# Moving the bias tile in front of the x tiles in a decoder-layer kernel

## The chip, the cores and the metric

The kernel runs on one core of one Trainium2 chip. The metric is the device time of one execution in microseconds (us): 1431.13 us, the median of three runs (1430.40 to 1431.53).

## What is computed

One decoder layer for 512 rows of 2048 values, in float32. One combined projection feeds three attention branches and three merge gates; the branches are projected back, gated, summed, projected once more and normalised:

```python
h = x @ w_in + b_in                       # 2048 -> 11528 columns
o_fox, o_swa, o_moba = fox(...), swa(...), moba(...)   # 8 heads of 64 each
br_i = (merge_heads(o_i) * silu(z_i)) @ w_branch_i     # 512 -> 2048, three times
y = sum_i sigmoid(gate_i) * br_i
out = y @ w_out                           # 2048 -> 2048
return layer_norm(alpha * x + out, ln_g, ln_b)
```

## The kernel before

**Number format.** Each float32 operand of a product is split into an upper part and a lower part, both of type float32r. A product of two split operands is three matmuls: upper by upper, upper by lower, lower by upper. A weight block of 128 partitions by 512 columns has the parts `hi` and `lo` (lines 132 and 135). x has `xh` and `xl`, the gated attention output `ozh` and `ozl`, and the mixed result y has `yh` and `yl`, which take over the buffers of `xh` and `xl` (tags `bigh` and `bigl`).

**The stream.** 452 weight blocks go through the kernel in one fixed order. They are loaded two at a time, and block i + 2 is split while block i is multiplied. In front of them stand two passes over the v columns. TensorE's work is this, with the stationary operand (the one loaded into the array) first:

- v passes, lines 272 to 274: a 128-column slice of `xh` or `xl` stays, 324 columns of `hi` or `lo` stream.
- projection `h`, lines 471 to 473: a 128-column slice of `hi` or `lo` stays, 512 columns of `xh` or `xl` stream. 81 tiles of 16 steps of three matmuls. The first 33 tiles belong to the attention branches, the last 48 are gates.
- moba v, lines 490 to 493: a slice of `xh` or `xl` stays, 256 columns of `hi` or `lo` stream.
- branch projections `br`, line 599: a slice of `hi` or `lo` stays, 512 columns of `ozh` or `ozl` stream. 36 matmuls follow each three gate tiles, and 72 stand at the end.
- output `o`, lines 650 to 652: a slice of `yh` or `yl` stays, 512 columns (in the last row tile 256) of `hi` or `lo` stream. The last eight blocks are kept in tiles of their own, `wh` and `wl`.

Attention runs in small steps put between the blocks of `h` and moba v: scores (lines 356 and 357, 96 units), transposes (line 398) and value products (line 417, 24 heads).

**Where tiles lie.** A pool's tiles are placed one behind the other in each partition, in the order of their first allocation, each rounded up to 32 bytes; a pool starts where the one before it ends. The pools are `keep`, `stage`, `ozy`, and behind them `const` and `work`, which give way first to `mix` and then to `last`. In `keep` stand `xh` and `xl` (32 KB each), `bT` and three tiles of 2 KB. `bT` holds the biases, 81 values per partition, 324 bytes, which take 352. All tiles of `stage` (raw blocks, `hi`, `lo`) and `ozy` are 2 KB or 4 KB. `ozh` and `ozl` (24 KB each) are the first tiles of `mix`. So, modulo 2 KB, everything in `stage`, `ozy` and the named tiles of `mix` lies 352 bytes behind `xh` and `xl`. In the built program `xh`, `xl`, `yh` and `yl` are at 128 modulo 2048, `hi`, `lo`, `ozh` and `ozl` at 480, and `wh` and `wl` at 928. A slice of 128 columns starts a multiple of 512 bytes further on.

PSUM has three accumulators of tag `acc` and five of tag `att`. `h` uses `acc`, `br` uses `att`, and `o` uses both.

Of the kernel before, what the change touches and what calls it, by code (L numbers as in the profile page):

```python
# [8 lines left out]
F32 = mybir.dt.float32  # L9
# [4 lines left out]
P = 128  # L14
# [14 lines left out]


def tile_columns():
    """Start columns of the 128-wide tiles of w_in whose product is kept transposed."""
    cols = []
    for p in range(4):
        cols += [FOX_Q + P * p, FOX_K + P * p, FOX_Z + P * p]
    cols.append(SWA_K)
    for p in range(4):
        cols += [SWA_Q + P * p, SWA_Z + P * p]
    for p in range(4):
        cols += [MOBA_Q + P * p, MOBA_K + P * p, MOBA_Z + P * p]  # L40
    for dt in range(KD):
        cols += [g + P * dt for g in GATES]
    return cols


# column ranges of the two v passes that run behind the loads of x
V_CHUNKS = (
    ((FOX_V, 320), (FOX_F, 4)),
    ((FOX_V + 320, 192), (SWA_V, 128), (FOX_F + 4, 4)),
# [2 lines left out]


def weight_stream():
    """The 512-column weight blocks in the order in which they are used."""
    ids = []
    t = 0

    def proj(n):
        nonlocal t  # L60
        for _ in range(n):
            ids.extend(("h", t, c) for c in range(4))
            t += 1

    proj(12)
    proj(1)
    for p in range(4):
        proj(2)
        if p % 2 == 1:
            ids.extend(("v", p // 2, g) for g in range(8))  # L70
    proj(12)
    proj(3)
    for dt in range(KD):
        if dt + 1 < KD:
            proj(3)
        ids.extend(("b", dt, b) for b in range(3))
    ids.extend(("o", ec, k) for ec in range(4) for k in range(KD))
    return ids
# [3 lines left out]
def hybrid_kernel(ctx: ExitStack, tc: tile.TileContext, a: dict, out: bass.AP):  # L82
# [4 lines left out]
    keep = ctx.enter_context(tc.tile_pool(name="keep", bufs=1))  # L87
# [4 lines left out]
    work = att_ctx.enter_context(tc.tile_pool(name="work", bufs=2))  # L92
# [10 lines left out]
        nc.scalar.activation(hi, raw, AF.Copy)  # L103
        nc.vector.tensor_sub(lo, raw, hi.bitcast(F32))  # L104

    # ---- the stream of weight blocks: loaded two at a time, split two blocks ahead of their use
    ids = weight_stream()
    raws, parts = {}, {}
    held = {}
# [8 lines left out]
            nc.sync.dma_start(raws[j], a["ws"][j])  # L118

    def prepare(i):  # L120
        """Rounds block i to its upper part; the step that is returned makes the lower part."""
        if i >= len(ids) or i in parts:
            return None
        load(i // 2)
        raw = raws[i // 2][:, (i % 2) * S:(i % 2 + 1) * S]
        if i in held:
            hi, lo = held[i]
        else:
            hi = stage.tile([P, S], F32R, tag="hi", name="hi")
            lo = stage.tile([P, S], F32R, tag="lo", name="lo")  # L130
        parts[i] = (hi, lo)
        nc.scalar.activation(hi, raw, AF.Copy)  # L132

        def lower():
            nc.vector.tensor_sub(lo, raw, hi.bitcast(F32))  # L135
            for d in range(1, raw_bufs):
                load(i // 2 + d)

        return lower

    # ---- x and the first two v passes
    xh = keep.tile([P, KD, S], F32R, tag="bigh", name="xh")
    xl = keep.tile([P, KD, S], F32R, tag="bigl", name="xl")
    bT = keep.tile([P, 81], F32, name="bT")
    sinkc = const.tile([P, NH], F32, name="sinkc")
    nsink = const.tile([P, NH], F32, name="nsink")
    vfox = const.tile([P, 4, NH, P], F32R, tag="v", name="vfox")
# [16 lines left out]
            nc.sync.dma_start(vraw[n][:, :2 * NV], a["wv"][n])  # L164

    def prepare_v(n):
        """Step n of 32: one block of the v columns, and one of x in the first pass."""
        hi = stage.tile([P, S], F32R, tag="hi", name="hi")
        lo = stage.tile([P, S], F32R, tag="lo", name="lo")
        split(vraw[n // 2][:, (n % 2) * NV:(n % 2 + 1) * NV], hi[:, :NV], lo[:, :NV])  # L170
        if n == 0:
            for c in (slice(0, 256), slice(256, S)):
                nc.vector.tensor_copy(xh[:, 0, c], xraw[0][:, c])
                nc.vector.tensor_sub(xl[:, 0, c], xraw[0][:, c], xh[:, 0, c].bitcast(F32))
        elif n < KD:
            split(xraw[n], xh[:, n], xl[:, n])
        vparts[n] = (hi, lo)
# [4 lines left out]
    load_v(1)  # L182
    load_v(2)

    # products of zeros wake the tensor engine while the first loads run
    warm = stage.tile([P, S], F32R, tag="hi", name="warm")
    nc.vector.memset(warm.bitcast(F32), 0.0)
    wacc = att_tile("warm")
# [39 lines left out]
                                 dst[:, st, h0:h0 + nh, :HD].bitcast(F32))  # L228

    def forget_bias():  # L230
        """8 times minus the running sum of the log-sigmoid; log1p(e) = 2 atanh(e / (2 + e))."""
        nlf = const.tile([P, 32], F32, name="nlf")
        fl = flog.rearrange("p a b -> p (a b)")
        t0 = const.tile([P, 32], F32, name="t0")
        t1 = const.tile([P, 32], F32, name="t1")
        t2 = const.tile([P, 32], F32, name="t2")
        nc.vector.scalar_tensor_tensor(t0, fl, -1.0, fl, op0=ALU.mult, op1=ALU.max)
        nc.scalar.activation(t0, t0, AF.Exp, scale=-1.0)
        nc.vector.tensor_scalar(t1, t0, 2.0, None, op0=ALU.add)
        nc.vector.reciprocal(t1, t1)  # L240
        nc.vector.tensor_mul(t0, t0, t1)
        nc.vector.tensor_mul(t1, t0, t0)
        nc.vector.tensor_scalar(t2, t1, 2.0 / 15.0, 2.0 / 13.0, op0=ALU.mult, op1=ALU.add)
        for c in (11, 9, 7, 5, 3, 1):
            nc.vector.tensor_mul(t2, t2, t1)
            nc.vector.tensor_scalar(t2, t2, 2.0 / c, None, op0=ALU.add)
        nc.vector.tensor_mul(t2, t2, t0)
        nc.vector.tensor_scalar(t1, fl, 0.0, None, op0=ALU.min)
        nc.vector.tensor_sub(nlf, t2, t1)
        pair = work.tile([P, 4, P], F32R, tag="L", name="pair", bufs=3)  # L250
        nc.gpsimd.memset(pair.bitcast(F32), 0.0)
        n3 = nlf.rearrange("p (a b) -> p a b", b=NH)
        nc.scalar.activation(pair[:, :, :NH], n3, AF.Copy)
        nc.vector.tensor_sub(pair[:, :, 32:32 + NH], n3, pair[:, :, :NH].bitcast(F32))
        return pair
# [38 lines left out]
        if KD + 1 <= n < KD + 5:  # L294
            v_evac(0, n - KD - 1, fox_dests[0])

    # ---- attention, in steps that run between the blocks of the projections
    halves = (slice(0, HD), slice(HD, P))

    def q_upper(acc, t, res):  # L300
# [129 lines left out]
    oz = []  # L430

    def plan_pair(kind, p, base, spacing, q, k, z, v):
        """Puts the steps of two heads into the slots from base on."""
        oz.append(z)
        for e in range(2):
            h = 2 * p + e
            g = p // 2 if kind == "swa" else e
            env = {"q": q, "k": k, "z": z, "v": v, "vh": g if kind == "swa" else h, "e": e, "g": g}
            first = base + int(4 * e * spacing)
            at(first - (4 if kind == "fox" else 0), 0, table_for, kind, h, env)  # L440
            for i in range(4):
                s = base + int((4 * e + i) * spacing)
                u = {}
                a_ = (kind, h, i, env, u)
                at(s, 8, unit_scores, *a_)
                at(s + 1, 0, unit_max, *a_)
                at(s + 1, 5, unit_exp, *a_)
                at(s + 2, 1, unit_norm, *a_)
                at(s + 3, 8, unit_turn, *a_)
                at(s + 4, 1, unit_upper, *a_)  # L450
                at(s + 4, 6, unit_lower, *a_)
            at(s + 6, 8, head_values, kind, h, env)
            at(s + 7, 2, head_low, kind, h, env)
            at(s + 7, 7, head_out, kind, h, env)
        return s + 7

    # ---- the parts of the stream
    where = {}
    for i, (kind, t, c) in enumerate(ids):
        where.setdefault((kind, t), i)  # L460
# [52 lines left out]
        nc.vector.tensor_sub(d[:, :, HD:], r, d[:, :, :HD].bitcast(F32))  # L513

    def evac(t, res, *steps):
        """The steps after tile t of the projection: slots after its last one, order there, function."""
        ends[t] = [(*x, res) for x in steps]

    Q = ((1, 2, q_upper), (2, 2, q_lower))
# [2 lines left out]
    t = 0  # L522
# [118 lines left out]
    oacc = {}  # L641

    def out_mm(st, k, hi, lo, half=None):
        """One block of the output product; half: only these 256 columns, in a bank of their own."""
        sl = slice(st * P, (st + 1) * P)
        o = oacc[st]
        if half is not None:
            cs = slice(half * 256, (half + 1) * 256)
            o, hi, lo = oacc[3 + half][:, :256], hi[:, cs], lo[:, cs]
        nc.tensor.matmul(o, yb["h"][:, k, sl], hi, start=(k == 0), stop=False)  # L650
        nc.tensor.matmul(o, yb["l"][:, k, sl], hi, start=False, stop=False)  # L651
        nc.tensor.matmul(o, yb["h"][:, k, sl], lo, start=False, stop=(k == KD - 1))  # L652
# [23 lines left out]
                at(i + 1, 1, residual, ec, st, oacc[st])  # L676

    def norm(st, middle=None):
        """Layer norm of one row tile: columns up to cut on VectorE, the others on ScalarE and GpSimdE."""
        last = st == 3  # L680
        cut = 1536 if last else 1024
        mv = box["last"].tile([P, 5], F32, tag="mv", name="mv", bufs=2)
# [35 lines left out]
            nc.sync.dma_start(rows[:, 2 * S:cut], z[:, 2 * S:cut])  # L718
        nc.sync.dma_start(rows[:, cut:], z[:, cut:])

    # ---- extra work at given slots
    for st in range(4):
        at(st, 3, v_evac, 1, st, fox_dests[1])
    nl = {}
# [93 lines left out]
```

## Time and profile before

| | |
|---|---|
| three runs | 1430.40, 1431.13, 1431.53 us |
| span of the profiled execution | 1429.3 us (1.8 us less than the median run) |
| TensorE matmuls | busy 1409.2 us, 99%, 6659 matmuls |
| weight loads | busy 1167.2 us, 82% |
| VectorE, ScalarE, GpSimd | 45%, 39%, 10% |
| granted TensorE clock, mean | 0.996 of full speed |

The busy time of a matmul (0.39 to 0.40 us at 512 columns) overlaps that of the next, which starts some 0.23 us after it. What a stream of matmuls costs is therefore read from start to start, and called the period here.

### The profile page before, as it was taken

How to read it: one execution, taken by the hardware profiler on the slowest of the kernel's cores; microseconds unless marked ns; L12 is line 12 of the kernel's file. 1: busy time of each engine (PE TensorE's matmuls, PEld its weight loads, DVE VectorE, ACT ScalarE, POOL GpSimd, SP SyncE). 2: the span in 40 equal slices, each digit the busy share in tenths (PEclk: the TensorE clock that was granted, in tenths of full speed). 3: DMA queues.
4: the chain of work that ended last, by engine and by line, in shares of the span. 5: the costliest groups of instructions: out<-in, count | busy, mean ns of one | idle time of the engine just before them, and what ended most of it. 6: DMA issues, size and time to landing. Idle time of an engine off the chain costs nothing.

```text
span 1429.3 us, 17708 instructions
## 1 busy us (share of the span) xinstructions
PE 1409.2 (99%) x6659; PEld 1167.2 (82%) x6659; DVE 636.7 (45%) x1273; ACT 556.8 (39%) x1024; POOL 150.1 (10%) x216
## 2 busy tenths in 40 slices
PE   9999999999999999999999999999999999999995
PEld 8988888898988888888888888888888888888884
DVE  5466656544554555442233333233333323632348
ACT  4355566555545556532222222222222222422231
POOL 1001212332321222100000000000000000000005
PEclk9999999999999999999999999999999999999998
DMA  7333223222222222232323323233232332362322
GB/s 240 116 102 102 82 89 95 75 79 89 79 74 89 89 74 75 81 96 89 103 89 93 99 89 104 89 92 100 89 103 89 92 100 89 119 249 91 101 74 118
DMA packets 41157, 142.37 MB, mean 100 GB/s; under 512 B 4632, under 2 KB 5144, under 8 KB 40304
## 3 DMA queue, kind: packets, MB, share of 16 engines
q1 hardware_dynamic: 40048, 134.58, 30.1%
q0 software_dynamic: 1024, 6.67, 1.2%
q8 instruction: 52, 0.85, 0.2%
q14 instruction: 33, 0.27, 0.1%
HBM read 137.02 MB, written 4.21 MB: 99 GB/s over the span
## 4 chain that ended last, share of the span: by engine, by line
PE 97%; DVE 2%; DMA 1%; SPq 0%; DVEq 0%; issue 0%; ACT 0%
PE h L471 21%; PE h L473 21%; PE h L472 21%; PE br L599 9%; PE o L651 4%; PE o L650 4%; PE o L652 4%; PE o L417 2%; PE pt L398 2%; PE mv L490 1%; PE mv L492 1%; PE mv L493 1%; PE s L357 1%; PE s L356 1%; PE vc L273 1%; PE vc L272 1%
## 5 line engine op out<-in xcount | busy, mean ns | idle before, releaser
L132 ACT ACTIVATE hi<-raw 128x512 fp32r<-128x512 f32 x444 | 280.2, 631 | 740.9 <-PE h L472 464.6
L135 DVE TENSOR_TENSOR lo<-raw,hi 128x512 fp32r<-128x512 f32 x444 | 312.7, 705 | 565.3 <-ACT hi L132 556.7
L471 PE MATMUL h<-xh,hi 128*128 128x512 f32 x1296 | 515.3, 398 | 0.0
L473 PE MATMUL h<-xh,lo 128*128 128x512 f32 x1296 | 513.9, 397 | 0.0
L472 PE MATMUL h<-xl,hi 128*128 128x512 f32 x1296 | 513.3, 396 | 0.0
L473 PEld LDWEIGHTS h<-xh,lo 128*128 128x128 f32 x1296 | 244.0, 188 | 59.4 <-DVE lo L135 0.3
L472 PEld LDWEIGHTS h<-xl,hi 128*128 128x128 f32 x1296 | 244.3, 188 | 55.8
L471 PEld LDWEIGHTS h<-xh,hi 128*128 128x128 f32 x1296 | 244.0, 188 | 55.4
L393 POOL TENSOR_SCALAR lt<-lt,st 128x128 f32<-128x128 f32 (+2 forms) x96 | 70.1, 730 | 309.7 <-DVE st L392 308.0
L651 PE MATMUL o<-hi,yl 128*128 128x512 f32 (+1 forms) x232 | 90.7, 391 | 0.0
L650 PE MATMUL o<-hi,yh 128*128 128x512 f32 (+1 forms) x232 | 89.6, 386 | 0.0
L652 PE MATMUL o<-lo,yh 128*128 128x512 f32 (+1 forms) x232 | 89.2, 384 | 0.0
L599 PE MATMUL br<-ozl,hi 128*128 128x512 f32 x192 | 74.9, 390 | 0.0
L599 PE MATMUL br<-ozh,hi 128*128 128x512 f32 x192 | 74.8, 390 | 0.0
L599 PE MATMUL br<-ozh,lo 128*128 128x512 f32 x192 | 74.7, 389 | 0.0
L631 POOL DMA_DIRECT2D z<-in_xn x4 | 2.2, 550 | 642.1 <-DVE yl L104 642.1
L387 ACT ACTIVATE lt<-lt,st 128x128 f32<-128x128 f32 (+3 forms) x96 | 51.4, 536 | 23.4 <-DVE st L392 10.4
L650 PEld LDWEIGHTS o<-hi,yh 128*128 128x128 f32 x232 | 43.5, 188 | 10.6
L652 PEld LDWEIGHTS o<-lo,yh 128*128 128x128 f32 x232 | 43.5, 188 | 9.6
L651 PEld LDWEIGHTS o<-hi,yl 128*128 128x128 f32 x232 | 43.6, 188 | 9.4
L405 ACT ACTIVATE pth<-pt 128x128 fp32r<-128x128 f32 (+2 forms) x96 | 38.6, 402 | 15.0 <-PE pt L398 14.2
L409 DVE TENSOR_TENSOR ptl<-pt,pth 128x128 fp32r<-128x128 f32 (+2 forms) x96 | 43.4, 452 | 1.0 <-ACT pth L405 0.7
(156 smaller groups left out, 1430.4 us busy)
## 6 DMA issues: line engine op xcount, KB each, us to landing
raw<-in_ws SPq DMA_DIRECT2D x226, 512.0 KB, 3.5
rawv<-in_wv SPq DMA_DIRECT2D x15, 324.0 KB, 3.2
xraw<-in_xT SPq DMA_DIRECT2D x16, 256.0 KB, 5.7
z<-in_xn POOLq DMA_DIRECT2D x4, 1024.0 KB, 9.8
out<-z SPq DMA_DIRECT2D x7, 512.0 KB, 2.6
row<-forget_rows SPq DMA_DIRECT2D x8, 256.0 KB, 3.8
ln_gain<-in_ln_gain POOLq DMA_DIRECT2D x1, 1024.0 KB, 17.9
ln_bias<-in_ln_bias POOLq DMA_DIRECT2D x1, 1024.0 KB, 20.3
```

The source lines that it names most:

```text
L132: nc.scalar.activation(hi, raw, AF.Copy)
L135: nc.vector.tensor_sub(lo, raw, hi.bitcast(F32))
L387: nc.scalar.activation(full[:, :m], full[:, :m], AF.Exp, bias=st[:, 0:1], scale=-1.0, accum_out=st[:, 1:2])
L393: nc.gpsimd.tensor_scalar(lt, lt, st[:, 3:4], 1.0, op0=ALU.mult, op1=ALU.mult)
L409: nc.vector.tensor_sub(env["ptl"][:, c], u["pt"][:, :u["n"] // P], env["pth"][:, c].bitcast(F32))
L471: nc.tensor.matmul(accs[t], hi[:, cc], xh[:, k], start=(k == 0), stop=False)
L472: nc.tensor.matmul(accs[t], hi[:, cc], xl[:, k], start=False, stop=False)
L473: nc.tensor.matmul(accs[t], lo[:, cc], xh[:, k], start=False, stop=(k == KD - 1))
L599: nc.tensor.matmul(br, w[:, cc], o[:, 4 * b + kt], start=(kt == 0 and n == 0), stop=(kt == 3 and n == 2))
L650: nc.tensor.matmul(o, yb["h"][:, k, sl], hi, start=(k == 0), stop=False)
L651: nc.tensor.matmul(o, yb["l"][:, k, sl], hi, start=False, stop=False)
L652: nc.tensor.matmul(o, yb["h"][:, k, sl], lo, start=False, stop=(k == KD - 1))
```

## The change

The tile `bT` is allocated as the first tile of the pool `keep`, no longer behind `xh` and `xl`. In the built program `bT` is then at 128 modulo 2048, and `xh`, `xl`, `yh` and `yl` at 480, where `hi`, `lo`, `ozh` and `ozl` have been and stay. `wh` and `wl` stay at 928. No other tile moves. The instructions of every engine, their order and their shapes are the same before and after, row for row. The rest of the diff turns comments and docstrings into empty lines and is left out here.

```diff
+    bT = keep.tile([P, 81], F32, name="bT")
     xh = keep.tile([P, KD, S], F32R, tag="bigh", name="xh")
     xl = keep.tile([P, KD, S], F32R, tag="bigl", name="xl")
-    bT = keep.tile([P, 81], F32, name="bT")
     sinkc = const.tile([P, NH], F32, name="sinkc")
```

## Rows read from the trace of the kernel before

**Rows 1.** The page: busy time by engine (us, share, instructions), and PE's shares by slice.
```profile
PE 1409.2 (99%) x6659; PEld 1167.2 (82%) x6659; DVE 636.7 (45%) x1273; ACT 556.8 (39%) x1024; POOL 150.1 (10%) x216
...
PE   9999999999999999999999999999999999999995
...
PEclk9999999999999999999999999999999999999998
```

**Rows 2.** Waits of PE and PEld: waiter, waited for: us in total, times, longest.
```profile
PE warm L190 <- DVE warm L187: 1.5, 1, 1.5
PE va L272 <- ACT xh L103: 0.7, 1, 0.7
PE va L273 <- DVE xl L104: 0.5, 2, 0.3
...
PEld h L473 <- DVE lo L135: 0.3, 1, 0.3
```

**Rows 3.** The chain that ended last, gate stage: start us, us, what.
```profile
713.26 8.19 PE br L599 x36
...
755.18 8.19 PE br L599 x36
...
1216.22 16.35 PE br L599 x72
```

**Rows 4.** Timeline of PE where br begins: start us, us, engine, line, operation, tiles.
```profile
713.10 0.39 PE L599 MATMUL br<-ozh,hi 128*128 128x512 f32 x1
713.33 0.40 PE L599 MATMUL br<-ozl,hi 128*128 128x512 f32 x1
713.57 0.39 PE L599 MATMUL br<-ozh,lo 128*128 128x512 f32 x1
...
714.26 0.39 PE L599 MATMUL br<-ozh,lo 128*128 128x512 f32 x1
...
715.85 0.39 PE L599 MATMUL br<-ozh,hi 128*128 128x512 f32 x1
```

**Rows 5.** Timeline of PE in the output product, 180 matmuls apart.
```profile
1284.91 0.39 PE L650 MATMUL o<-hi,yh 128*128 128x512 f32 x1
...
1326.91 0.39 PE L650 MATMUL o<-hi,yh 128*128 128x512 f32 x1
```

**Rows 6.** Groups by line and form: xcount | busy us, mean ns | idle before.
```profile
L471 PE MATMUL h<-xh,hi 128*128 128x512 f32 x1296 | 515.3, 398 | 0.0
...
L650 PE MATMUL o<-hi,yh 128*128 128x512 f32 x216 | 85.1, 394 | 0.0
...
L490 PE MATMUL mv<-hi,xh 128*128 128x256 f32 x128 | 36.6, 286 | 0.0
...
L272 PE MATMUL vc<-hi,xh 128*128 128x324 f32 x64 | 20.1, 314 | 0.0
...
L650 PE MATMUL o<-wh,yh 128*128 128x512 f32 x24 | 9.5, 395 | 0.0
```

**Rows 7.** Timeline of PE in the v passes, 192 matmuls apart.
```profile
23.80 0.31 PE L272 MATMUL va<-hi,xh 128*128 128x324 f32 x1
...
52.59 0.31 PE L272 MATMUL vc<-hi,xh 128*128 128x324 f32 x1
```

**Rows 8.** Timeline of PE in moba v, 23 matmuls apart.
```profile
303.32 0.28 PE L490 MATMUL mv<-hi,xh 128*128 128x256 f32 x1
...
306.07 0.29 PE L493 MATMUL mv<-lo,xh 128*128 128x256 f32 x1
```

**Rows 9.** Groups by line and form: steps that stand between matmuls of h.
```profile
L356 PEld LDWEIGHTS s<-kh,qs 128*128 128x128 f32 x96 | 18.2, 189 | 2.5
...
L423 ACT ACTIVATE otmp<-o 64x512 f32<-64x512 f32 x24 | 14.3, 594 | 2.9 <-PE o L417 2.4
```

**Rows 10.** Groups by line: the splits of the weight blocks.
```profile
L132 ACT ACTIVATE hi<-raw 128x512 fp32r<-128x512 f32 x444 | 280.2, 631 | 740.9 <-PE h L472 464.6
L135 DVE TENSOR_TENSOR lo<-raw,hi 128x512 fp32r<-128x512 f32 x444 | 312.7, 705 | 565.3 <-ACT hi L132 556.7
```

**Rows 11.** Busy time in a stretch of gate tiles: us, count; clock, DMA share, GB/s.
```profile
721.45:755.18 33.73, 33.73 (x145) 27.12 (x145) 9.62 (x14) 8.75 (x15) 0.00 (x0) 1.00 0.30 94
```

**Rows 12.** Timeline of PE at a score step: 384 columns, `kh` and `qs` at equal offsets.
```profile
169.09 0.27 PE L398 MATMUL pt<-ident,lt 128*128 128x128 f32 x1
169.12 0.42 PE L356 MATMUL s<-kh,qs 128*128 128x384 f32 x1
169.38 0.34 PE L357 MATMUL s<-kl,qs 128*128 128x384 f32 x1
169.55 0.40 PE L471 MATMUL h<-xh,hi 128*128 128x512 f32 x1
```

**Rows 13.** Timeline at the end: the last matmul.
```profile
1411.65 0.28 PE L652 MATMUL o<-wl,yh 128*128 128x256 f32 x1
```

## The prediction

> **What bounds the kernel now.** Read the page first: PE is busy 1409.2 of 1429.3 us, every slice but the last shows 9, and its clock is granted in full (9 in all slices but the last) [rows 1]. Then the waits: PE waits 2.7 us for anything in the whole program, all of it in the first microseconds, and its weight loads wait once for a split inside the stream, 0.3 us [rows 2]. So neither a transfer nor another engine holds the stream back. What counts is how long one matmul takes from start to start. Busy time does not tell that, since neighbours overlap; the starts do.
>
> For `h`, take the chain in the gate stage: 36 matmuls of `br` from 713.26, lasting 8.19 us, and the next 36 at 755.18 [rows 3]. Between them are three gate tiles, 144 matmuls, in 755.18 - 713.26 - 8.19 = 33.73 us: a period of 0.2342 us. For `br`, the last group has 72 matmuls in 16.35 us [rows 3]. Its second half, less a first half like the other groups, takes 16.35 - 8.19 = 8.16 us for 36: 0.2267 us. Both kinds have 128x512 operands, three matmuls per step and the same clock. `h` is 3.3% slower.
>
> What sets them apart? Not the array of weights or its buffers: both load `hi` and `lo` from the same tiles. Not the PSUM tag: `o` uses both tags, and its period is (1326.91 - 1284.91) / 180 = 0.2333 us [rows 5], near `h`. What `br` has alone is that its streaming operand (480 modulo 2048) and its stationary operand (480 plus a multiple of 512) lie at equal offsets modulo 512. In `h` they lie 352 bytes apart, in `o` the same with the parts exchanged, and with `wh` and `wl` 800. A second sign is the entry into `br`: the first five periods take (714.26 - 713.10) / 5 = 0.232 us, the next seven (715.85 - 714.26) / 7 = 0.227 [rows 4]. The short period is a rhythm into which streaming and loading fall after some matmuls, and which `h` and `o` never find.
>
> I read this as two reads of the same memory that get in each other's way less often when both walk through it in step. The trace shows the periods, not this cause. The Trainium skill speaks against it: "SBUF — State Buffer", section "Who interferes with whom", gives PE two independent read ports and says that PE never waits on anyone. By that the offset would be worth nothing, and `h` and `br` would have one period; the measured 0.2342 against 0.2267 differ, so the trace does not agree with it as it stands.
>
> **The change, part by part.** No instruction, DMA or wait is added, removed or moved. `bT` itself is read as one value per partition by ScalarE and VectorE, which have time to spare (39% and 45% busy [rows 1]). What changes is that x and y go to 480 modulo 2048. `h`, `o` (but for `wh` and `wl`), moba v and the v passes then have both operands at equal offsets modulo 512, as `br` has now.
>
> 1. Gate tiles of `h`: 48 tiles of 48 matmuls, 2304 in all. Each goes from 0.2342 to 0.2267, saving 0.0075 us: 17.3 us. The rhythm then also runs through the 15 entries into `br` that now cost 8.19 - 8.16 = 0.03 us each: 0.4 us more. Together 17.7 us.
> 2. The other 1296 x 3 - 2304 = 1584 matmuls of `h` [rows 6] would save 11.9 us by the same step. But attention steps break in: 96 score units (mostly with a transpose right before them) and 24 value products [rows 9], up to 120 interruptions. After each the rhythm must be found again; the price is that of the entry into `br`, 0.03 us. 120 x 0.03 = 3.6 us, which leaves 8.3 us. Bounds: 0, if the rhythm never returns in so short a run, and 11.9.
> 3. `o` with `hi` and `lo` at 512 columns: 3 x 216 = 648 matmuls [rows 6], 0.2333 - 0.2267 = 0.0066 us each: 4.3 us. The 72 with `wh` and `wl` [rows 6] go from 800 to 448 bytes apart, unequal before and after: nothing, at most 72 x 0.0066 = 0.5.
> 4. v passes and moba v: 384 matmuls of 324 columns and 384 of 256 (six lines of 64 and three of 128 [rows 6]). Their periods are 28.79 / 192 = 0.150 us [rows 7] and 2.75 / 23 = 0.120 us [rows 8]. No row shows narrower matmuls at equal offsets in a steady run. The upper bound is a saving per column like that of `h`: 0.0047 x 384 = 1.8 and 0.0038 x 384 = 1.4, together 3.2 us. The lower bound is nothing, if what is left over does not shrink with the width. I take the middle, 1.6 us.
>
> The other engines' cover: splits of a block cost ScalarE 0.631 and VectorE 0.705 us [rows 10], against 12 x 0.2267 = 2.72 us for a block of PE's work afterwards, and most of the idle time before the upper split is a wait for PE to free a buffer [rows 10]. A faster PE starts it earlier. If that cover were gone, the 0.3 us wait of [rows 2] shows what a late split costs, once. DMA is busy 30% in the gates at 94 GB/s [rows 11]; 3% more is no load. The tail, from the last matmul at 1411.65 [rows 13] to 1429.3, is VectorE's, GpSimd's and a store's, and stays.
>
> Sum: 17.7 + 8.3 + 4.3 + 1.6 = 31.9 us. The profiled span of 1429.3 becomes 1397.4. The median run is 1431.1, 1.8 above the span, so the time becomes **1399 us**. With every bound at its best (17.7 + 11.9 + 0.5 + 4.3 + 3.2 = 37.6) it is 1393.5.
>
> **The rivals.**
>
> *The offset is not what matters.* The short period of `br` would belong to where `ozh` and `ozl` lie in the whole partition, not modulo 512. For it: no row shows x at another offset. Against it: `o` streams `hi` and `lo`, or `wh` and `wl`, which lie in a distant part of the partition, and both have the same line times (394 and 395 ns [rows 6]); only `br` stands out. Time 1431. By the section of the Trainium skill named above ("SBUF — State Buffer", "Who interferes with whom") nothing would change either, with the same 1431; that rule has [rows 3] against it.
>
> *The rhythm holds only in long undisturbed runs.* Between attention steps there are often only 12 to 18 matmuls of `h`. If the rhythm is not found there, terms 2 and 4 fall to nothing: 17.7 + 4.3 = 22.0 us saved, 1409 us. For it: five periods are lost at each entry into `br` [rows 4], where only one operand changes. Against it: five are a third of such a run, no more.
>
> *Equal offsets collide.* Both reads would hit the same place at the same moment, and the change makes `h` slower. For it: a score matmul whose `kh` and `qs` lie at equal offsets takes 169.38 - 169.12 = 0.26 us for 384 columns, and the next one, of the same width, 0.17 [rows 12]. Against it: a transpose starts 0.03 us earlier and still runs in that time, and `br` has equal offsets and the shortest period of all. As price I take the slowest step of the entry into `br`, 713.57 - 713.33 = 0.24 us [rows 4], an estimate from rows rounded to 0.01. If `h` stayed at 0.24, 3888 x 0.0058 = 22.6 us more: 1454. It decides once the period of `h` rises by 2.9 / 3888 = 0.0007 us.
>
> **How the numbers follow.** A change under 0.2%, 2.9 us, can't be told from none. Chances: the forecast, 1393 to 1405, 0.68; the rhythm only in long runs, 1405 to 1412, 0.14; no effect, 0.12; collision, 0.04; more than my best bounds, 0.02. The range from 1392 to 1412 takes in the first two, with the unknown costs of terms 2 and 4, and leaves out what gives no gain. Faster by over 0.2%: 0.68 + 0.14 + 0.02 = 0.84. Within 0.2%: 0.12. Slower: 0.04.
>
> **What would show it.** In the changed profile, the 144 matmuls of `h` between two groups of `br` should take 32.6 us, not 33.7, and each group of `br` 8.16. 180 matmuls of `o` should take 40.8 us, not 42.0. In the attention stage the starts of `h` should be 0.23 to 0.24 us apart for some five matmuls after a score step and 0.227 after that. PE's waits should stay at a few microseconds. The prediction is wrong if `h` keeps 0.234 (then place or another cause counts), or if new waits of PE for splits or for attention steps eat what the period gives back.

## The result and the profile after

The changed kernel takes 1400.07 us (median of four runs, 1399.89 to 1401.47), the kernel before 1431.24 (median of four). The ratio is 0.9784, with a 95% interval of 0.9772 to 0.9796: 2.2% faster. The profiled execution took 1399.89 us with a span of 1398.1, so 1.8 us lie around the span, as before.

The page of the changed kernel, first its busy times by engine, then the granted clock by slice:

```profile
PE 1377.4 (99%) x6659; PEld 1162.8 (83%) x6659; DVE 636.3 (46%) x1273; ACT 556.8 (40%) x1024; POOL 151.4 (11%) x216
...
PEclk9999999999999999999999999999999999999998
```

Against [rows 1], PE is 31.8 us less busy with the same 6659 matmuls, and VectorE, ScalarE and GpSimd have changed by at most 1.3 us. The clock is granted as before. Its waits (waiter, waited for, us in total, times, longest):

```profile
PE warm L190 <- DVE warm L187: 1.5, 1, 1.5
PE va L272 <- ACT xh L103: 0.8, 1, 0.8
PE va L273 <- DVE xl L104: 0.6, 2, 0.3
...
PEld h L473 <- DVE lo L135: 0.5, 1, 0.5
```

These are the waits of [rows 2], longer by 0.4 us in all. So nothing was won by a wait that went, and no new wait has come. The matmuls themselves follow each other faster. The chain that ended last, at the groups of `br` (start us, us, what):

```profile
618.01 8.16 PE br L599 x36
658.81 8.16 PE br L599 x36
699.61 8.16 PE br L599 x36
...
1189.21 16.32 PE br L599 x72
```

The 144 matmuls of `h` between two groups take 658.81 - 618.01 - 8.16 = 32.64 us: a period of 0.2267, where [rows 3] gave 0.2342. `br` takes 8.16 in every group; its slow entry is gone. In the output product, with 186 matmuls between these two:

```profile
1259.77 0.39 PE L650 MATMUL o<-hi,yh 128*128 128x512 f32 x1
...
1301.93 0.39 PE L650 MATMUL o<-hi,yh 128*128 128x512 f32 x1
```

42.16 / 186 = 0.2267, where [rows 5] gave 0.2333. The last matmul of all now starts here:

```profile
1380.29 0.28 PE L652 MATMUL o<-wl,yh 128*128 128x256 f32 x1
```

The first group of `br` in the kernel before, from the same view as [rows 3]:

```profile
629.44 8.18 PE br L599 x36
```

By stage, with the starts of the first and the last group of `br` as borders:

| stretch | before | after | less |
|---|---|---|---|
| start to the first group of `br` | 629.44 | 618.01 | 11.43 |
| to the last group (14 times 144 `h` and 36 `br`) | 586.78 | 571.20 | 15.58 |
| to the last matmul | 195.43 | 191.08 | 4.35 |
| from there to the end of the span | 17.7 | 17.8 | -0.1 |

### The profile page after: what moved, and what is told of

The parts are those of the page before. It is cut to its first block, busy times and chain, and to the rows that moved or that the text cites. A ratio compares the mean times of both kernels' runs of the same rounds, so it can differ in the third digit from the quotient of the medians.

```text
span 1398.1 us, 17708 instructions
## 1 busy us (share of the span) xinstructions
PE 1377.4 (99%) x6659; PEld 1162.8 (83%) x6659; DVE 636.3 (46%) x1273; ACT 556.8 (40%) x1024; POOL 151.4 (11%) x216
## 4 chain that ended last, share of the span: by engine, by line
PE 96%; DVE 2%; DMA 1%; SPq 0%; issue 0%; ACT 0%; DVEq 0%; ACTq 0%
PE h L471 21%; PE h L473 21%; PE h L472 21%; PE br L599 9%; PE o L651 4%; PE o L650 4%; PE o L652 4%; PE o L417 2%; PE pt L398 2%; PE mv L490 1%; PE mv L492 1%; PE mv L493 1%; PE s L357 1%; PE s L356 1%; DMA xraw<-in_xT 1%; PE vc L274 1%
## 5 line engine op out<-in xcount | busy, mean ns | idle before, releaser
L471 PE MATMUL h<-xh,hi 128*128 128x512 f32 x1296 | 507.4, 392 | 0.0
L473 PE MATMUL h<-xh,lo 128*128 128x512 f32 x1296 | 505.1, 390 | 0.1
L472 PE MATMUL h<-xl,hi 128*128 128x512 f32 x1296 | 505.2, 390 | 0.0
```

The source lines that it names most:

```text
L471: nc.tensor.matmul(accs[t], hi[:, cc], xh[:, k], start=(k == 0), stop=False)
L472: nc.tensor.matmul(accs[t], hi[:, cc], xl[:, k], start=False, stop=False)
L473: nc.tensor.matmul(accs[t], lo[:, cc], xh[:, k], start=False, stop=(k == KD - 1))
```

## The experiments

Four questions were put to the chip: how near must the offsets be; is it the offset between the two operands, or the place of x; what is the rest of a period lost to; and can the attention steps join. A period of `h` below is always that of 144 matmuls between two groups of `br`, as above.

### How near must the offsets be?

Four kernels have the changed order and a gap behind the x tiles, of 64, 32, 8 and 120 values (256, 128, 32 and 480 bytes):

```diff
     xl = keep.tile([P, KD, S], F32R, tag="bigl", name="xl")
+    keep.tile([P, 64], F32, name="gap")
```

> A gap of 256 bytes behind the x tiles moves the weight parts and the attention output on, so that in h, o and the v passes the two operands lie 256 bytes apart modulo 512; br stays at 0. Theory 1 (only equal offsets modulo 512 give the short period): h at 0.233 to 0.235 us, br at 0.2267, time about 1430. Rival (the walk repeats every 256 bytes or less): h stays at 0.2267, time about 1400. Rival (what counts is that x starts at 480 modulo 2048): h stays at 0.2267, time about 1400.

> As gap_256 with 128 bytes. Theory 1: h at 0.233 to 0.235 us, time about 1430. Rival (repeats every 128 bytes): h at 0.2267, time about 1400, and then gap_256 the same. Rival (x at 480 counts): 0.2267, about 1400.

> As gap_256 with 32 bytes, the smallest step of the placing. Theory 1, strict: h at 0.233 to 0.235 us, time about 1430. Theory 1 with some play (near enough to equal is as good): h at 0.2267, time about 1400; gap_480, 32 bytes short of the next 512, then tells whether the play is on one side or both.

> As gap_256 with 480 bytes, that is 32 bytes the other way. Theory 1, strict: h at 0.233 to 0.235 us, time about 1430. With play on both sides: 0.2267 and about 1400, as gap_32. Rival (x at 480 counts): 0.2267, about 1400.

One execution each: 1401.14, 1425.15, 1425.03 and 1426.53 us, in this order; the kernel before took 1431.45 beside them. The chain of gap_256, then of gap_128, gap_32 and gap_480:

```profile
700.76 8.16 PE br L600 x36
741.56 8.16 PE br L600 x36
```

```profile
709.56 8.18 PE br L600 x36
751.32 8.17 PE br L600 x36
```

```profile
708.73 8.18 PE br L600 x36
750.51 8.19 PE br L600 x36
```

```profile
710.10 8.20 PE br L600 x36
751.90 8.20 PE br L600 x36
```

The periods of `h` are 32.64 / 144 = 0.2267, then 33.58 / 144 = 0.2332, and 33.60 / 144 = 0.2333 twice. So 32 bytes to either side cost the rhythm, 128 do, and 256 do not. Equality modulo 512 was too strict: 256 is enough, 128 is not. That x starts at 480 modulo 2048 falls as an explanation, since it did so in all four.

Not every unequal offset costs the whole step. In gap_128 the last eight blocks, `wh` and `wl`, are at 1056 and `yh` and `yl` at 480 in the built program, 64 bytes apart modulo 256. 71 periods lie between these two rows:

```profile
1383.23 0.39 PE L651 MATMUL o<-wh,yh 128*128 128x512 f32 x1
...
1399.49 0.40 PE L653 MATMUL o<-wl,yh 128*128 128x512 f32 x1
```

16.26 / 71 = 0.2290, between 0.2267 and 0.2333. The three slow kernels are still 5 to 6 us faster than the kernel before: 0.2333 is not 0.2342 (3888 x 0.0009 = 3.5 us of that), so which unequal offset it is has an effect of its own.

### The offset, or the place?

One kernel keeps the tile order of before, with the bias tile padded to 512 bytes (of which the kernel uses 81 values, as ever), so that x is at 128 and the weight parts at 640. The other has the order of after, and moves `ozh` and `ozl` alone of the tiles that TensorE reads (two kinds of tiles behind them in `mix`, `sig` and `y`, move along):

```diff
-    bT = keep.tile([P, 81], F32, name="bT")
+    bT = keep.tile([P, 128], F32, name="bT")[:, :81]
```

```diff
+        mix.tile([P, 40], F32, name="gap")
         box["ozh"] = mix.tile([P, 12, S], F32R, name="ozh")
```

> The tile order of before, x at 128 modulo 2048, but the bias tile is padded to 512 bytes, so that the weight parts and the attention output lie at 640, equal to x modulo 512. Theory 1 (the offset between the operands counts): h, o and br at 0.2267 us, time 1400, ratio 0.978. Rival (x has to be at 480, or the bias tile has to stand in front): h stays at 0.234, time 1431, ratio 1.000. Rival (equality modulo 2048 is needed, not 512): 1431 too, with br alone short.

> The changed kernel with a gap of 160 bytes in front of the attention output's split parts, which puts them against the weight parts as x was before the change. Theory 1: br rises to 0.234 us, 576 x 0.0075 = 4.3 us more than the changed kernel, 1404, ratio 0.981; h and o stay at 0.2267. Rival (the place of the attention output in the partition makes br short): br stays at 0.2267 and the time at 1400, ratio 0.978.

Padding alone, with the bias tile where it was: 1400.19 us, ratio 0.9784 (0.9768 to 0.9800), the same as the change. Moving `ozh` and `ozl` away: 1405.29 us, ratio 0.9818 (0.9804 to 0.9833). The chain of the first, then of the second:

```profile
701.06 8.16 PE br L599 x36
741.86 8.16 PE br L599 x36
```

```profile
660.20 8.43 PE br L600 x36
701.28 8.43 PE br L600 x36
...
1194.33 16.86 PE br L600 x72
```

With the padding the period of `h` is 32.64 / 144 = 0.2267. With `ozh` and `ozl` moved, `br` takes 16.86 / 72 = 0.2342 us, the period that `h` had before the change, and `h` stays at (701.28 - 660.20 - 8.43) / 144 = 0.2267. (Its profiled run took 1405.68 us, 5.8 more than that of the changed kernel. Summed from start to start, 4.30 of them are in `br` and 1.34 in the v passes, which come up again below.) The same matmuls get slow or fast with nothing changed but 160 bytes between their operands. This shows the offset as the cause, for `br` by taking it away and for `h` by both ways of making it equal. The place in the partition is out as a rival.

### What is the rest of a period lost to?

The expectations below set a period against 0.2133 us, which is 512 columns at one per cycle of 2.4 GHz. No run here shows a period that short, so this is an assumption of theirs; by it 0.0133 of a period of 0.2267 are the rest, and 0.0209 of one of 0.2342. Two pairs of kernels load and use only 64 of the 128 weight columns in `h`: one pair in the second matmul of each three, the other in all but the first and last step of a tile. Both do so on the kernel before and on the changed one.

```diff
-            nc.tensor.matmul(accs[t], hi[:, cc], xl[:, k], start=False, stop=False)
+            half = slice(j * P, j * P + 64)
+            nc.tensor.matmul(accs[t][:64], hi[:, half], xl[:, k], start=False, stop=False)
```

```diff
+            n = P if k in (0, KD - 1) else 64
+            half, acc = slice(j * P, j * P + n), accs[t][:n]
-            nc.tensor.matmul(accs[t], hi[:, cc], xh[:, k], start=(k == 0), stop=False)
+            nc.tensor.matmul(acc, hi[:, half], xh[:, k], start=(k == 0), stop=False)
...
```

> The changed kernel, in which the second of each three matmuls of h (upper weight part by lower x part) loads and uses only the first 64 of 128 weight columns; half of that product is left out. Theory 1 with its cause (what a period has over 512 columns at full clock, 0.2267 - 0.2133 = 0.0133 us, is lost to the weight load that runs beside the streaming): the period in which the half load runs shrinks by about half of that, 0.0067 us, so 1296 x 0.0067 = 8.7 us less, 1391. Rival (the 0.0133 us belong to the switch from one matmul to the next, whatever is loaded): no period changes, 1400.

> The kernel before, with the same half load; half of that product is left out. There a period has 0.2342 - 0.2133 = 0.0209 us over the 512 columns. Theory 1 with its cause: the period with the half load beside it shrinks by about 0.0104 us, 1296 x 0.0104 = 13.5 us, 1418. Rival (lost to the switch): no period changes, 1431.

> The changed kernel, in which all matmuls of h but those of the first and last step of a tile load and use only 64 of the 128 weight columns (half of those products is left out). Theory 1 with its cause (the time over 512 columns is lost to the load beside the streaming; half_after was slow because loads of two lengths alternated and broke the rhythm): periods of 0.2200 us inside a tile, 3402 x 0.0067 = 22.7 us less, 1377. Rival (lost to the switch of matmuls): 0.2267, 1400. Rival (the rhythm needs loads of full length): 0.230 or more, 1410 or more.

> The kernel before with the same half loads in h. Theory 1 with its cause: the 0.0209 us over 512 columns fall to about half, periods of 0.2238, 3402 x 0.0104 = 35 us less, 1395. Rival (lost to the switch): 0.2342, 1431. If only the conflict of the two reads shrinks and a fixed part stays, something between.

One execution each: 1410.02 and 1423.39 us with one load in three halved, 1409.55 and 1417.22 with all of them. The changed kernel gets 10 us slower by loading less, the kernel before 7 and 14 us faster. With one load in three halved, all three periods of a step rise in the changed kernel, to 0.2289, 0.2304 and 0.2300 on average in the gates, and not only the one beside the half load. In the second pair, the chain of the changed kernel's, then of the other:

```profile
704.15 8.16 PE br L601 x36
745.38 8.16 PE br L601 x36
```

```profile
706.39 8.17 PE br L601 x36
747.73 8.17 PE br L601 x36
```

The loads did become shorter (groups by line, the changed kernel; mean ns of one behind the comma):

```profile
L474 PEld LDWEIGHTS h<-xl,hi 128*64 128x64 f32 x1134 | 152.5, 134 | 101.4
...
L474 PEld LDWEIGHTS h<-xl,hi 128*128 128x128 f32 x162 | 30.5, 188 | 6.0
```

Of 144 matmuls 18 keep the full load. With those at 0.2267 and 0.2342, the other 126 take (33.07 - 18 x 0.2267) / 126 = 0.2301 us in the changed kernel and (33.17 - 18 x 0.2342) / 126 = 0.2298 in the other. Read from start to start, two neighbours with half loads are 0.2300 and 0.2298 us apart, two with full loads 0.2267 and 0.2342, as without the edit. With half loads the offset no longer counts: both stand between the two periods of the full load. My theory that the excess is in proportion to what is loaded falls, and so does its rival, that it belongs to the switch from one matmul to the next. The third reading, that the rhythm needs loads of full length, foretold 0.230 or more and 1410 us or more; 0.2301 and 1409.55 came. What stays is that halving the load changes the period, in both directions. It also halves the rows of the result, and no run parts the two. Whether two reads of the memory get in each other's way, and how, is open.

### Can the attention steps join?

The last two kernels of the study compare the changed kernel with one in which the attention tiles lie at 480 modulo 512 too, as x and the weight parts do. Only their order and one gap differ (the lines further down that allocated `ident`, `causal` and `band` go):

```diff
-    sinkc = const.tile([P, NH], F32, name="sinkc")
-    nsink = const.tile([P, NH], F32, name="nsink")
     vfox = const.tile([P, 4, NH, P], F32R, tag="v", name="vfox")
     vswa = const.tile([P, 4, 2, P], F32R, name="vswa")
+    ident = const.tile([P, P], F32, name="ident")
+    causal = const.tile([P, P], F32, name="causal")
+    band = const.tile([P, 256], F32, name="band")
+    const.tile([P, 80], F32, name="gap")
+    sinkc = const.tile([P, NH], F32, name="sinkc")
+    nsink = const.tile([P, NH], F32, name="nsink")
...
```

> The changed kernel with the attention tiles (v, scores' q and k, transposed weights, work rows) placed at equal offsets modulo 512 with x and the weight parts as well; order and work unchanged. Theory 1 (an interruption costs the rhythm only because its operands lie at other offsets): most of the 3.6 us that the interruptions of h cost is saved, time 1397, ratio 0.976, and h next to a score step is at 0.227 at once. Rival (other widths and the transposes break the rhythm whatever their offsets): no change, 1400, ratio 0.978.

> The changed kernel once more, beside align_att on the same chip, to compare the two: 1400, ratio 0.978 by every theory. If the v passes fall into one of two rhythms by chance, single runs lie near 1400.0 or near 1401.5.

1399.85 us with a ratio of 0.9778 (0.9764 to 0.9791), and 1399.95 us with 0.9779 (0.9766 to 0.9792): no difference in time. The 1584 matmuls of `h` in the attention stage, summed from start to start, take 363.62 us in the aligned kernel and 363.86 in the changed one. The timeline of the aligned kernel behind a score step:

```profile
166.43 0.39 PE L472 MATMUL h<-xh,hi 128*128 128x512 f32 x1
...
167.82 0.39 PE L472 MATMUL h<-xh,hi 128*128 128x512 f32 x1
168.04 0.39 PE L473 MATMUL h<-xl,hi 128*128 128x512 f32 x1
...
168.95 0.39 PE L474 MATMUL h<-xh,lo 128*128 128x512 f32 x1
```

The first six periods take 1.39 / 6 = 0.232 us, the four from 168.04 on 0.91 / 4 = 0.2275. The rhythm is lost at a score step although the operands lie at equal offsets. Something else in the step is enough, be it the other widths or the transpose; the runs don't part these. The rival's forecast of the time, no change, holds.

The value products, though, do join where they have 512 columns. Their operands were 128 bytes apart and are equal in the aligned kernel. The first of two such products and the matmul behind the second, in the aligned kernel and in the changed one:

```profile
169.18 0.39 PE L418 MATMUL o<-pth,vfox 128*128 128x512 f32 x1
...
169.63 0.33 PE L418 MATMUL o<-pth,vfox 128*128 128x384 f32 x1
```

```profile
168.94 0.39 PE L417 MATMUL o<-pth,vfox 128*128 128x512 f32 x1
...
169.40 0.34 PE L417 MATMUL o<-pth,vfox 128*128 128x384 f32 x1
```

0.45 / 2 = 0.225 us against 0.46 / 2 = 0.230; over all 32 of them it is 0.2267 against 0.2311. This is 0.15 us in all, too little to show in the time.

The second kernel also showed something about the v passes. In the profile of the changed kernel 138 periods lie between the first two of these rows; in its second profile 135 lie between the other two:

```profile
29.71 0.31 PE L273 MATMUL va<-hi,xl 128*128 128x324 f32 x1
...
49.95 0.31 PE L273 MATMUL vc<-hi,xl 128*128 128x324 f32 x1
```

```profile
29.71 0.31 PE L273 MATMUL va<-hi,xl 128*128 128x324 f32 x1
...
49.88 0.31 PE L273 MATMUL vc<-hi,xl 128*128 128x324 f32 x1
```

20.24 / 138 = 0.1467 us and 20.17 / 135 = 0.1494, by the same program. At 324 columns the matmuls fall into one rhythm or another from run to run; [rows 7] gave 0.150. Summed from start to start, the second v pass takes 28.16 us in the first profile and 28.67 in the second; the first pass, which waits for x at its start, takes 31.22 and 31.13. So the rhythm is worth some 0.5 us, and it does not explain why single runs of the changed kernel differ by up to 1.6 us: the two runs took 1399.89 and 1399.95. Nor do the five runs of the second kernel, 1399.43 to 1400.59, fall into two groups. The v passes as a whole can differ by more: in the profiled run of the padded kernel, 1401.56 us, they take 61.06 us, and 59.38 in that of the changed one, 1399.89. The other runs were not profiled.

## Why the prediction held

The forecast was 1399 us with a range of 1392 to 1412, the measured median 1400.07. Its steps:

- **Gates, 17.7 us.** The middle stretch of the table holds 2016 of the 2304 gate matmuls and 14 of the 15 entries: 2016 x 0.0075 + 14 x 0.03 = 15.5 us were forecast for it, 15.58 measured. The whole term is a little smaller than forecast: summed from start to start, all 2304 gate matmuls save 16.75 us and `br` 0.38, together 17.1. Attention steps still break into the first six gate tiles twelve times, and the prediction had counted these tiles as undisturbed. Both rows named ahead came: 32.6 us for 144 matmuls of `h`, 8.16 for a group of `br`.
- **`h` in the attention stage, 8.3 us.** Summed from start to start over the whole trace, these 1584 matmuls take 372.14 us before and 363.86 after: 8.28 less. The price of the interruptions was right in size, and the rhythm comes back in short runs. The timeline of the changed kernel behind a score step shows it, at 0.23 for some eight periods and not five:

```profile
166.18 0.40 PE L471 MATMUL h<-xh,hi 128*128 128x512 f32 x1
...
168.03 0.39 PE L473 MATMUL h<-xh,lo 128*128 128x512 f32 x1
...
168.71 0.39 PE L473 MATMUL h<-xh,lo 128*128 128x512 f32 x1
```

  (168.03 - 166.18) / 8 = 0.231, then (168.71 - 168.03) / 3 = 0.227.
- **`o`, 4.3 us.** The stretch from the last group of `br` to the last matmul gives 4.35, of which 0.03 are the entry into that group. Summed from start to start, the 648 matmuls take 151.20 us before and 147.08 after, 4.12 less. The 72 with `wh` and `wl` take 16.79 and 16.81: nothing, as forecast. The half blocks of the last row tile, 256 columns wide, gave the other 0.2; the prediction had left them out.
- **v passes and moba v, 1.6 us.** Summed in the same way, the v passes take 60.93 before and 59.38 after, moba v 46.53 and 46.37: 1.7 us together. That this is near the forecast is partly luck. Moba v at 256 columns gained almost nothing. The v passes gained 1.55 between these two profiles, but in the changed kernel's second profile and in those of the other kernels with equal operands they take 59.80 to 61.06, and the 60.93 of before lie within that. How much of it the offset earns is not shown.
- **The cover.** Waits grew by 0.4 us in all: 0.2 for x at the start and 0.2 for the one late split, where the prediction had named it. The tail is some 0.1 us longer.

The rivals: that the place counts fell by oz_off and both_128. With it falls what the prediction had drawn from the Trainium skill, that the offset would be worth nothing because PE's two read ports are independent ("SBUF — State Buffer", section "Who interferes with whom"): 160 bytes between the operands make `br` 0.2342 instead of 0.2267. Where in PE this arises no run shows, and whether PE ever waits on another engine's reads was not tested. That the rhythm holds only in long runs fell by the 8.28 us above. That equal offsets collide fell by every run with equal offsets.

One step of the reasoning was too strict: "equal offsets modulo 512". The runs show that 256 bytes are as good as none. So the prediction had the right condition for the short period, the offset between the two operands, and nearly the right sizes. Its picture of the cause, two reads in step, is not shown: the runs say only that halving the load changes the period too, and that the excess is not in proportion to what is loaded.

## What to carry to other kernels

Where TensorE is busy all the time, compare periods from start to start between kinds of matmuls of one shape. If they differ without a wait, look at the offsets of their streaming and stationary tiles: here float32r operands of 512 columns ran 3% faster at equal offsets modulo 256, and one padded small tile was enough to get there. A small tile allocated among large ones shifts everything behind it; pad it, or put it where it shifts both operands alike.

## What was not expected

- At 256 columns equal offsets are not best. The last row tile's half blocks have `wh` and `wl` at 928 and `yh` and `yl` at 480, which is 192 bytes modulo 256, and 40 periods end with the last matmul shown above:

```profile
1375.76 0.28 PE L651 MATMUL o<-wh,yl 128*128 128x256 f32 x1
```

  (1380.29 - 1375.76) / 40 = 0.1133 us. Moba v, of the same width and at equal offsets, stays at 46.4 / 384 = 0.121 us with its few interruptions. In gap_32, at 32 bytes, moba v takes 45.39 us, 1.0 less than at equal offsets.
- Loading half as many weights in `h` made the changed kernel slower by 10 us.
